# Small matmul groups of the mixers: fewer pauses between their halves, and row halves in alternation

## The chip, the cores and the metric

The kernel runs on one core of a Trainium2 chip. The metric is the device time of one execution in microseconds (us), from three runs of the kernel before: median 1280.27, lowest 1278.59, highest 1280.76. The engines of the core run side by side, each through its own instructions in program order: PE (TensorE, the matmuls), DVE (VectorE), ACT (ScalarE), POOL (GpSimd) and SP (which issues most DMAs). They wait for each other at semaphores.

## The reference

Two layers over 256 tokens of width 1024. Each layer adds half a SwiGLU FFN, a mixer and half a second FFN to the residual; a final RMSNorm follows. Cut to what matters here:

```python
for l in range(DEPTH):                      # DEPTH = 2
    x = x + 0.5 * swiglu(rmsnorm(x, ffn1_norm[l]), ...)
    h = rmsnorm(x, mix_norm[l])
    p = h @ w_in[l]                         # 1024 -> 8*256 + 4*1024
    u_a, u_b, r_p, k_p, v_p, z_in, b_g, c_g, gate_pre = jnp.split(p, SPLIT_POINTS, axis=-1)
    y_a = s5_mixer(u_a, ...)                # state space model, 16 groups
    y_b = pool_mixer(u_b, ...)
    y_c = rwkv7_mixer(h, r_p, k_p, v_p, ...)   # 4 heads of 64, delta rule
    y_d = short_conv_mixer(z_in, b_g, c_g, ...)
    branches = jnp.einsum('bsgc,gcd->bsgd', ys, w_branch[l])
    x = x + jnp.sum(branches * gates, axis=2).reshape(...) @ w_out[l]
    x = x + 0.5 * swiglu(rmsnorm(x, ffn2_norm[l]), ...)
return rmsnorm(x, final_norm)
```

`rwkv7_mixer` needs low-rank products for its decay, its learning rate and its gate, and a recurrence over time, which the kernel computes in four chunks of 64 tokens with small matrices for each head and chunk.

## The kernel before

**The main line.** Every large product (FFN, input projection, gates, branches, output) is made of float32r matmuls of 128 by 128 weights with 512 columns. A float32 operand is split into a high and a low part, so that each k-tile takes three matmuls (lines 256, 257, 258). I call these three a **tick**; the code calls `fl.tick()` after each. The weights come as units of two k-tiles: a DMA to `raw`, a conversion to `wh` on ACT (line 250), and the rest `wl` on DVE (line 225, the line of a helper that records every `tensor_tensor`).

**The side threads.** The mixer's branches are Python generators that are resumed between ticks while the program is being written, so the order of each engine's instructions is fixed by their `yield`s. `wA(n)` resumes before the products of the n-th step on (a step is two ticks of the same unit). `wM(n, banks)` resumes n ticks on, one such thread per tick, and only when so many of the four PSUM banks of the small products are free in this count. `Flow.tick` and `Flow._run` (lines 93 to 136) do this. An engine never leaves its order: what stands first and waits holds up all that is behind it.

**The small groups.** Between the ticks of each mixer PE also runs groups of small float32 matmuls. Names in the order in which they come, with the line of the matmul:

- `lr` (945): low-rank outputs, contraction over 64 rows for the first two and over 128 for the third; 256 columns each, two matmuls a group.
- `sT` (1352), `sY` (1397): input and output of S5. `sY` multiplies `U8` with `LK`, then the states `Hs` with `CA`, for four values of `u`.
- `gm` (1064): pair matrices of the four heads. Contraction over 64 rows: the upper half of the partitions for even heads, the lower half for odd ones. Its operands are `BK` and `W`. DVE masks the result into `Gm`; then POOL copies its diagonal blocks to `dg`, four copies per head (1073), and builds `Bl` and `Rd` from `dg`.
- `tmA`, `tmB` (1114, 1115): eight full transposes; DVE copies `tmA` to `RH`.
- `akv` (1138), `inv` (1093, 1171, 1183), `wu` (1202), `mq` (1228, 1229), `pn` (1243), `po` (1250), `zc` (1264), `pqz` (1282): the chunk recurrence, with 64 by 64 or 32 by 32 pieces.

Most of these groups are cut in two, three or four by a `yield wM()` in the middle of the loop: part, tick, part. The states `Hs` of S5 are made by DVE scans over `gB` and `gA`, two products on POOL (`gA`, `gB`), and a subtraction on DVE.

Of the kernel before, what the change touches and what calls it, by code (L numbers as in the profile page):

```python
# [50 lines left out]
def wA(n=1):  # L51
    """Resume before the products of the step n steps on."""
    return ("A", n, 0)


def wC(n=1):
    """As wA, after the conversion of weights."""
    return ("C", n, 0)


def wB(n=0, banks=0):
    """Resume after the products of the step n steps on, with so many PSUM banks free."""
    return ("B", n, banks)


def wT(n=1):
    """Resume n ticks on; a tick is between the products of two k-tiles."""
    return ("T", n, 0)


def wM(n=1, banks=0):
    """As wT, for products: one such thread goes on per tick, with so many PSUM banks free."""
    return ("M", n, banks)


class Flow:
    """Program order: a main line of product steps, and side threads resumed between them."""
# [94 lines left out]
def trunk_kernel(ctx: ExitStack, tc: tile.TileContext, a, out, dbg=None):  # L172
# [17 lines left out]
    # ------------------------------------------------------------- constants  # L190
# [16 lines left out]
    # ------------------------------------------------------------- helpers  # L207
# [22 lines left out]
    class Unit:  # L230
        """A block of weights: [128, nk, n] loaded, then split into two float32r parts."""
# [44 lines left out]
    # ------------------------------------------------------------- residual update and norm  # L276
# [20 lines left out]
    def next_input(t, hf, p, scale, ss, gain):  # L297
        """Thread: half hf of the residual of token tile t, its transpose times the next norm's gain in
        two parts, its sum of squares; the norm's factor follows with the second half and is applied
        to the products."""  # L300
# [23 lines left out]
    def last_norm(t, hf, p, scale, ss):  # L324
        """Thread: half hf of the result of token tile t; the second half scales both by the norm's factor."""
# [67 lines left out]
    # ------------------------------------------------------------- FFN  # L393
# [75 lines left out]
    # ------------------------------------------------------------- parameter columns  # L469
# [9 lines left out]
    def load_vecs(i, vr, first, after):  # L479
        """Thread: the rows of a group of parameters, as columns of vec."""  # L480
# [34 lines left out]
    # ------------------------------------------------------------- S5 preparation  # L515
# [120 lines left out]
    def s5_prepare(l, tp):  # L636
        """Matrices of layer l: boundary input LS, boundary output CA, in-block LK, phasor tables."""
# [16 lines left out]
        # B rows (re | im) and swapped; C rows, to be transposed  # L654
# [9 lines left out]
        # powers a^0..a^8  # L664
# [27 lines left out]
        # phasor tables e^{i theta 8 b}  # L692
# [14 lines left out]
        # B-bar rows (re | im) and swapped  # L707
# [11 lines left out]
        # C rows: X1 = (cre | -cim), X2 = (cim | cre)  # L719
# [70 lines left out]
    # ------------------------------------------------------------- mixer  # L790
    def mixer(l):
# [34 lines left out]
        def cols(names, mk):  # L826
            """512 columns of products with the layer input; then as two banks [128 ch, 2, S]."""
# [29 lines left out]
        class LowRank:  # L857
            """Rows of the low-rank input weights, and those times mu, side by side."""
# [42 lines left out]
        # ------------------------------------------------------- RWKV  # L901
        def rwkv():
# [19 lines left out]
            # low-rank outputs  # L922
# [18 lines left out]
            for i, (o_, nm) in enumerate(((sig, "rwkv_w0"), (aa, "rwkv_a0"), (gg, None))):  # L941
                yield wM(2 if i else 6, 1)
                p = bank("lr").rearrange("p (j t) -> p j t", j=2)
                for j in range(2):
                    pe.matmul(p[:, j], lhsT=lw[rows[i], i // 2, j * 128:(j + 1) * 128], rhs=z[rows[i], i // 2],  # L945
                              start=True, stop=True)
                yield wA(1)
                if nm:
                    for j in range(2):
                        sc.activation(o_[:, j], p[:, j], AF.Sigmoid, bias=col(l, nm, j))  # L950
                else:
                    sc.activation(o_, p, AF.Copy)
                free()
# [8 lines left out]
            # normalised removal key  # L962
# [35 lines left out]
            # decay products within chunks  # L998
# [28 lines left out]
            # scaled operands; slots: even chunk (a, v, r), odd chunk (v, a, r)  # L1027
# [23 lines left out]
            # pair matrices, [s, t]; rows (b|k) for even chunks, (k|b) for odd ones; columns (a | r)  # L1051
# [3 lines left out]
            for h in range(4):  # L1055
                yield wM(4 if h == 0 else 2, 1)
                j, e = h // 2, h % 2
                es = slice(64 * e, 64 * e + 64)
                p = bank("gm").rearrange("p (c t) -> p c t", c=4)
                for c in range(4):  # L1060
                    m, o = c // 2, c % 2
                    lhs = BK[es, 2 * j + m, 2 * o:2 * o + 2].rearrange("p k t -> p (k t)")
                    rhs = W[es, 2 * j + m, 0:3:2] if o == 0 else W[es, 2 * j + m, 4:6]
                    pe.matmul(p[:, c], lhsT=lhs, rhs=rhs, start=True, stop=True)
                yield wA(1)
                g_ = et([128, 4, 128], f"Gm{h}")
                tt(g_, p, maskb)
# [169 lines left out]
            for c in range(3):  # L1237
                if c:
                    yield wM()
# [447 lines left out]
```

## Time and profile before

| | |
|---|---|
| median of 3 runs | 1280.27 us |
| span of the profiled execution | 1278.3 us |
| PE busy | 1255.6 us (98%) |
| DVE, ACT, POOL busy | 760.9, 618.8, 388.5 us |
| mixer of layer 0 / of layer 1, up to the end of `pqz` | about 215 to 392 / 845 to 1021 us |

The profiled execution's own time is its span and what lies around it; the span is 2.0 us under the median of the runs. A busy share is time in which at least one instruction of the engine ran. Matmuls are pipelined, so the start times of the timeline tell more than the busy time: the main line's matmuls start 0.23 us apart, and a tick is 0.68 us.

### The profile page before, as it was taken

Reading aid. Unit: us, or ns where it says so; the run is one execution under the profiler, and the core shown is the slowest. Engines: PE = TensorE matmul, PEld = TensorE weight load, DVE = VectorE, ACT = ScalarE, POOL = GpSimd, SP = SyncE. Lnnn points to the kernel's source line nnn. Section 1 sums busy time; section 2 is a strip of 40 time slices with the busy share of each in tenths; the row PEclk is TensorE's granted clock in tenths of the full one; section 3 lists DMA queues with packets and bytes.
Section 4 is the critical chain, followed back from the end, with each engine's and each line's share of the span. In section 5 each row is a group of like instructions: output and inputs, shape, how many; then the busy total and the mean of one; then the engine's idle time right before and its main releaser. Section 6 shows DMA issues by size and latency. Waiting matters only on the chain.

```text
span 1278.3 us, 19253 instructions
## 1 busy us (share of the span) xinstructions
PE 1255.6 (98%) x7472; PEld 1013.3 (79%) x7472; DVE 760.9 (60%) x935; ACT 618.8 (48%) x787; POOL 388.5 (30%) x512
## 2 busy tenths in 40 slices
PE   7999999999999999999999999999999999999997
PEld 6888878876777788888888788878677787888886
DVE  6956557497547565554465565465965476655543
ACT  5454435655334454444354444365554354544433
POOL 4694383263123210000069453204612032000001
PEclk9999999998999999999999999999999999999999
DMA  8665656543444566656666566555244455666561
GB/s 257 179 219 179 184 159 183 166 135 121 126 133 145 176 182 187 191 176 188 190 187 195 170 186 188 153 188 178 96 134 133 133 165 165 212 184 180 182 197 66
DMA packets 139667, 216.29 MB, mean 169 GB/s; under 512 B 30092, under 2 KB 42232, under 8 KB 139576
## 3 DMA queue, kind: packets, MB, share of 16 engines
q1 hardware_dynamic: 138296, 213.63, 54.9%
q10 hardware_dynamic: 1120, 1.40, 0.3%
q8 instruction: 58, 0.95, 0.3%
q0 software_dynamic: 160, 0.05, 0.1%
q14 instruction: 33, 0.27, 0.1%
HBM read 212.29 MB, written 1.57 MB: 167 GB/s over the span
## 4 chain that ended last, share of the span: by engine, by line
PE 94%; DVE 4%; issue 0%; DMA 0%; ACT 0%; SPq 0%; POOLq 0%; POOL 0%; DVEq 0%; ACTq 0%
PE acc L256 29%; PE acc L258 28%; PE acc L257 28%; PE pb L268 3%; DVE wl L225 1%; PE inv L1093 1%; DVE cv L1506 1%; PE lr L945 0%; DMA x<-in_x_dram 0%; PE sY L1397 0%; DVE Gm L225 0%; PE wu L1202 0%; PE pb L771 0%; DVE mg L225 0%; PE po L1250 0%
## 5 line engine op out<-in xcount | busy, mean ns | idle before, releaser
L225 DVE TENSOR_TENSOR wl<-raw,wh 128x1024 fp32r<-128x1024 f32 (+1 forms) x390 | 492.2, 1263 | 300.0 <-ACT wh L250 297.7
L250 ACT ACTIVATE wh<-raw 128x1024 fp32r<-128x1024 f32 (+1 forms) x393 | 414.6, 1055 | 425.4 <-PE acc L258 390.7
L256 PE MATMUL acc<-wh,xh 128*128 128x512 f32 (+1 forms) x1248 | 494.7, 396 | 0.0
L258 PE MATMUL acc<-wh,xl 128*128 128x512 f32 (+1 forms) x1248 | 475.1, 381 | 0.0
L257 PE MATMUL acc<-wl,xh 128*128 128x512 f32 (+1 forms) x1248 | 474.5, 380 | 0.1
L256 PEld LDWEIGHTS acc<-wh,xh 128*128 128x128 f32 x1248 | 235.6, 189 | 49.1 <-issue 6.8
L258 PEld LDWEIGHTS acc<-wh,xl 128*128 128x128 f32 x1248 | 235.6, 189 | 45.5
L257 PEld LDWEIGHTS acc<-wl,xh 128*128 128x128 f32 x1248 | 236.1, 189 | 39.1 <-DVE wl L225 0.6
L258 PE MATMUL acc<-wh,hl 128*128 128x512 f32 x352 | 138.7, 394 | 0.0
L256 PE MATMUL acc<-wh,hh 128*128 128x512 f32 x352 | 138.2, 393 | 0.0
L257 PE MATMUL acc<-wl,hh 128*128 128x512 f32 x352 | 138.0, 392 | 0.0
L225 POOL TENSOR_TENSOR wl<-raw,wh 128x1024 fp32r<-128x1024 f32 x11 | 26.4, 2396 | 239.9 <-ACT wh L250 239.9
L256 PEld LDWEIGHTS acc<-wh,hh 128*128 128x128 f32 x352 | 66.1, 188 | 15.2 <-issue 1.3
L257 PEld LDWEIGHTS acc<-wl,hh 128*128 128x128 f32 x352 | 66.2, 188 | 14.6
L258 PEld LDWEIGHTS acc<-wh,hl 128*128 128x128 f32 x352 | 66.2, 188 | 13.3
L429 DVE SCALAR_TENSOR_TENSOR hd<-acc,rs,sg 128x512 f32<-128x512 f32 (+1 forms) x48 | 33.7, 703 | 38.4 <-PE acc L258 36.5
L333 POOL TENSOR_SCALAR pre<-ss 128x1 f32<-128x1 f32 x2 | 0.4, 221 | 173.7 <-ACT junk L281 173.7
L221 ACT ACTIVATE hh<-pb 128x512 fp32r<-128x512 f32 (+1 forms) x48 | 27.0, 563 | 45.5 <-PE pb L268 45.5
L222 DVE TENSOR_TENSOR hl<-pb,hh 128x512 fp32r<-128x512 f32 (+1 forms) x48 | 31.0, 646 | 27.9 <-ACT hh L221 27.6
L422 ACT ACTIVATE sg<-acc,rs 128x512 f32<-128x512 f32 (+1 forms) x48 | 31.1, 654 | 17.8 <-PE acc L258 16.8
L225 POOL TENSOR_TENSOR mg<-mg,gate 128x512 f32<-128x512 f32 x16 | 28.6, 1807 | 13.5 <-DVE gate L225 13.5
L314 ACT ACTIVATE xh<-xg 128x512 fp32r<-128x512 f32 x24 | 15.2, 632 | 30.6 <-DVE xg L225 30.5
(341 smaller groups left out, 1131.9 us busy)
## 6 DMA issues: line engine op xcount, KB each, us to landing
raw<-in_w_in_dram SPq DMA_DIRECT2D x96, 512.0 KB
raw<-in_ffn_w_up_dram SPq DMA_DIRECT2D x88, 512.0 KB
raw<-in_ffn_w_down_dram SPq DMA_DIRECT2D x88, 512.0 KB
raw<-in_ffn_w_gate_dram SPq DMA_DIRECT2D x87, 512.0 KB
raw<-in_w_branch_dram SPq DMA_DIRECT2D x16, 512.0 KB
raw<-in_w_out_dram SPq DMA_DIRECT2D x16, 512.0 KB
x<-in_x_dram SPq DMA_DIRECT2D x2, 512.0 KB
raw<-in_rwkv_g_dram SPq DMA_DIRECT2D x8, 128.0 KB
```

The costliest lines, as they stand in the source:

```text
L221: sc.activation(dh, src, AF.Copy)
L222: eng.tensor_tensor(out=dl, in0=src, in1=dh.bitcast(F32), op=ALU.subtract)
L225: eng.tensor_tensor(out=o, in0=i0, in1=i1, op=op)
L250: sc.activation(self.h, self.r, AF.Copy)
L256: pe.matmul(ps, lhsT=lh, rhs=wh, start=first, stop=False)
L257: pe.matmul(ps, lhsT=lh, rhs=wl, start=False, stop=False)
L258: pe.matmul(ps, lhsT=ll, rhs=wh, start=False, stop=last)
L268: pe.transpose(b[:, j * 128:(j + 1) * 128], src[:, j * 128:(j + 1) * 128], ident)
L314: sc.activation(dh, xg, AF.Copy)
L422: sc.activation(sg[:, :n], pg[:, :n], AF.Silu, scale=rstd[t])
L429: ve.scalar_tensor_tensor(out=hd[:, :n], in0=pu[:, :n], scalar=rstd[t], in1=sg[:, :n], op0=ALU.mult, op1=ALU.mult)
L1093: pe.matmul(p[qs, u], lhsT=lhs[qs, u], rhs=rhs[qs, u], start=True, stop=True)
```

## The change

It changes the order in which small products are written, and nothing in what is computed:

- in `akv`, `wu`, `mq`, `pn`, `pqz` and `sT` the `yield wM()` inside the loop goes, so that the parts stand behind each other; in `po` and `sY` four parts (of which `po` had two groups) become one and two;
- `lr`: the first two products share a turn, take two banks, and alternate between the row halves;
- `gm`: the heads come in pairs, two banks at once; the matmuls of the even and the odd head alternate, and `wM` is 4 for both pairs.

`inv` keeps its halves. Comments were removed too, so line numbers fall by a few.

```diff
-            for i, (o_, nm) in enumerate(((sig, "rwkv_w0"), (aa, "rwkv_a0"), (gg, None))):
-                yield wM(2 if i else 6, 1)
-                p = bank("lr").rearrange("p (j t) -> p j t", j=2)
+            for group in (((0, sig, "rwkv_w0"), (1, aa, "rwkv_a0")), ((2, gg, None),)):
+                yield wM(6 if group[0][0] == 0 else 2, len(group))
+                ps = [bank("lr").rearrange("p (j t) -> p j t", j=2) for _ in group]
                 for j in range(2):
-                    pe.matmul(p[:, j], lhsT=lw[rows[i], i // 2, j * 128:(j + 1) * 128], rhs=z[rows[i], i // 2],
-                              start=True, stop=True)
+                    for p, (i, _, _) in zip(ps, group):
+                        pe.matmul(p[:, j], lhsT=lw[rows[i], i // 2, j * 128:(j + 1) * 128], rhs=z[rows[i], i // 2],
+                                  start=True, stop=True)
...
-            for h in range(4):
-                yield wM(4 if h == 0 else 2, 1)
-                j, e = h // 2, h % 2
-                es = slice(64 * e, 64 * e + 64)
-                p = bank("gm").rearrange("p (c t) -> p c t", c=4)
+            for j in range(2):
+                yield wM(4 if j == 0 else 4, 2)
+                ps = [bank("gm").rearrange("p (c t) -> p c t", c=4) for _ in range(2)]
                 for c in range(4):
                     m, o = c // 2, c % 2
...
+                    for e in range(2):
+                        es = slice(64 * e, 64 * e + 64)
+                        lhs = BK[es, 2 * j + m, 2 * o:2 * o + 2].rearrange("p k t -> p (k t)")
+                        rhs = W[es, 2 * j + m, 0:3:2] if o == 0 else W[es, 2 * j + m, 4:6]
+                        pe.matmul(ps[e][:, c], lhsT=lhs, rhs=rhs, start=True, stop=True)
                 yield wA(1)
...
+                for e in range(2):
+                    h = 2 * j + e
+                    g_ = et([128, 4, 128], f"Gm{h}")
+                    tt(g_, ps[e], maskb)
+                    free()
...
             for h in range(4):
-                if h % 2 == 0:
-                    yield wM()
...
-                    if h2:
-                        yield wM()
...
-                    if j:
-                        yield wM()
...
             for c in range(3):
-                if c:
-                    yield wM()
...
-                if c % 2 == 0:
+                if c == 0:
                     yield wM()
...
-                if e:
-                    yield wM()
...
             for u in range(4):
-                if u == 2:
-                    yield wM()
...
             for u in range(4):
-                if u:
+                if u == 2:
                     yield wM()
```

What this does to the order of the built program, in layer 0; layer 1 has the same.

PE, at the pair matrices `gm`, between the transposes `bg` and `cg` of the input projection. Before:

```order
L823 MATMUL bg<-cst,tm 128x128 x4
L256 MATMUL acc<-wh,xh 128x512
L257 MATMUL acc<-wl,xh 128x512
L258 MATMUL acc<-wh,xl 128x512
L256 MATMUL acc<-wh,xh 128x512
L257 MATMUL acc<-wl,xh 128x512
L258 MATMUL acc<-wh,xl 128x512
L1064 MATMUL gm<-W,BK 128x128 x4
L256 MATMUL acc<-wh,xh 128x512
L257 MATMUL acc<-wl,xh 128x512
L258 MATMUL acc<-wh,xl 128x512
L823 MATMUL cg<-cst,tm 128x128 x4
```

After:

```order
L1066 MATMUL gm<-W,BK 128x128 x8
L256 MATMUL acc<-wh,xh 128x512
L257 MATMUL acc<-wl,xh 128x512
L258 MATMUL acc<-wh,xl 128x512
L823 MATMUL bg<-cst,tm 128x128 x4
L256 MATMUL acc<-wh,xh 128x512
L257 MATMUL acc<-wl,xh 128x512
L258 MATMUL acc<-wh,xl 128x512
L256 MATMUL acc<-wh,xh 128x512
L257 MATMUL acc<-wl,xh 128x512
L258 MATMUL acc<-wh,xl 128x512
L823 MATMUL cg<-cst,tm 128x128 x4
```

The first `gm` group has moved up by two ticks and the `bg` transposes, and holds two heads.

DVE, from the conversion behind `v` to `BK`, the last operand of `gm`. Before:

```order
L225 TENSOR_TENSOR wl<-raw,wh 128x1024
L1015 TENSOR_SCALAR kp<-aa,vec 128x256 x2
L1016 SCALAR_TENSOR_TENSOR kp<-kp,k 128x512
L1017 SCALAR_TENSOR_TENSOR bvec<-kk,aa 128x512
L1024 SCALAR_TENSOR_TENSOR rk<-r,vec,kp 128x256 x2
L225 TENSOR_TENSOR W<-kk,L_2551 128x4x2x64
L225 TENSOR_TENSOR wl<-raw,wh 128x1024
L225 TENSOR_TENSOR BK<-bvec,L_2552 128x4x2x64
L225 TENSOR_TENSOR W<-r,L_2551 128x8x64
L225 TENSOR_TENSOR BK<-kp,L_2552 128x4x128
```

After:

```order
L225 TENSOR_TENSOR wl<-raw,wh 128x1024
L225 TENSOR_TENSOR L_2543<-L_2542 128x512
L1017 TENSOR_SCALAR kp<-aa,vec 128x256 x2
L1018 SCALAR_TENSOR_TENSOR kp<-kp,k 128x512
L1019 SCALAR_TENSOR_TENSOR bvec<-kk,aa 128x512
L225 TENSOR_TENSOR wl<-raw,wh 128x1024
L1026 SCALAR_TENSOR_TENSOR rk<-r,vec,kp 128x256 x2
L225 TENSOR_TENSOR W<-kk,L_2542 128x4x2x64
L225 TENSOR_TENSOR BK<-bvec,L_2543 128x4x2x64
L225 TENSOR_TENSOR W<-r,L_2542 128x8x64
L225 TENSOR_TENSOR wl<-raw,wh 128x1024
L225 TENSOR_TENSOR BK<-kp,L_2543 128x4x128
```

Between `v` and `BK` there are now three conversions `wl`, where there were two; one that stood ahead of `v` has come behind it.

POOL, from the copies of the diagonal blocks to the products `gA` and `gB` for `Hs`; the number behind `Gm_` tells the heads apart. Before:

```order
L1073 COPY dg<-Gm_2706 32x64 x4
L1073 COPY dg<-Gm_2735 32x64 x4
L1073 COPY dg<-Gm_2756 32x64 x4
L1384 MEMSET Hs 128x16
L225 TENSOR_TENSOR gA<-gA,TC 128x512
L225 TENSOR_TENSOR gB<-gB,TS 128x512
L1073 COPY dg<-Gm_2783 32x64 x4
L225 TENSOR_TENSOR Bl<-dg,cst 128x256 x2
L225 TENSOR_TENSOR Rd<-Bl,cst 128x256
```

After:

```order
L1077 COPY dg<-Gm_2697 32x64 x4
L1077 COPY dg<-Gm_2703 32x64 x4
L1077 COPY dg<-Gm_2750 32x64 x4
L1077 COPY dg<-Gm_2756 32x64 x4
L225 TENSOR_TENSOR Bl<-dg,cst 128x256 x2
L225 TENSOR_TENSOR Rd<-Bl,cst 128x256
L1376 MEMSET Hs 128x16
L225 TENSOR_TENSOR gA<-gA,TC 128x512
L225 TENSOR_TENSOR gB<-gB,TS 128x512
```

The fourth head's copies, two `Bl` and `Rd` now stand ahead of `gA` and `gB`, with all 16 copies before them.

## Rows read from the trace of the kernel before

**Rows 1.** The page's chain by engine, and its group of weight conversions.
```profile
PE 94%; DVE 4%; issue 0%; DMA 0%; ACT 0%; SPq 0%; POOLq 0%; POOL 0%; DVEq 0%; ACTq 0%
...
L225 DVE TENSOR_TENSOR wl<-raw,wh 128x1024 fp32r<-128x1024 f32 (+1 forms) x390 | 492.2, 1263 | 300.0 <-ACT wh L250 297.7
```

**Rows 2.** Stretches, layers 0 and 1: busy PE, PEld, DVE, ACT, POOL; granted clock; DMA.
```profile
277.00:297.10 20.10, 16.81 (x96) 12.80 (x94) 19.96 (x27) 8.09 (x11) 13.43 (x20) 0.98 0.35 107
297.10:303.30 6.20, 6.16 (x39) 4.23 (x40) 2.57 (x4) 2.71 (x5) 2.29 (x4) 0.52 0.36 115
...
927.10:930.60 3.50, 3.19 (x28) 1.83 (x29) 2.05 (x5) 2.34 (x5) 2.56 (x4) 0.59 0.50 154
```

**Rows 3.** PE's timeline around `lr`: start us, length us, line, operation, last the idle time.
```profile
227.95 0.39 PE L258 MATMUL acc<-wh,xl 128*128 128x512 f32 x1
...
228.63 0.39 PE L258 MATMUL acc<-wh,xl 128*128 128x512 f32 x1
228.95 1.13 PE L945 MATMUL lr<-z,lw 64*128 64x256 f32 x4
...
230.58 0.39 PE L258 MATMUL acc<-wh,xl 128*128 128x512 f32 x1
...
233.91 0.39 PE L258 MATMUL acc<-wh,xl 128*128 128x512 f32 x1
234.13 1.02 PE L945 MATMUL lr<-z,lw 128*128 128x256 f32 x4
...
235.46 0.39 PE L258 MATMUL acc<-wh,xl 128*128 128x512 f32 x1
```

**Rows 4.** PE's timeline around a half of `akv`.
```profile
312.15 0.39 PE L258 MATMUL acc<-wh,yl 128*128 128x512 f32 x1
312.47 0.68 PE L1138 MATMUL akv<-UV,Gm 64*64 64x64 f32 x16
...
313.66 0.39 PE L258 MATMUL acc<-wh,yl 128*128 128x512 f32 x1
```

**Rows 5.** PE's timeline: the first `gm`, `tmA` between two ticks, the first `sY`.
```profile
277.85 1.13 PE L1064 MATMUL gm<-W,BK 64*128 64x128 f32 x8 [0.57 <-DVE BK L225]
...
291.37 0.40 PE L258 MATMUL acc<-wh,xl 128*128 128x512 f32 x1
...
292.94 0.40 PE L258 MATMUL acc<-wh,xl 128*128 128x512 f32 x1
...
293.96 0.43 PE L1397 MATMUL sY<-LK,U 128*32 128x128 f32 x8
297.14 0.66 PE L1397 MATMUL sY<-CA,Hs 128*32 128x128 f32 x8 [2.76 <-DVE Hs L225]
```

**Rows 6.** DVE's timeline from `v` to `Hs`.
```profile
262.79 0.87 DVE L917 SCALAR_TENSOR_TENSOR v<-v,vec 128x255 f32<-128x255 f32 x2 [0.16 <-ACT v L915]
...
277.03 0.68 DVE L225 TENSOR_TENSOR BK<-kp,L 128x512 f32<-128x512 f32 x1
...
281.88 0.69 DVE L225 TENSOR_TENSOR Gm<-gm,cst 128x512 f32<-128x512 f32 x1
...
296.38 0.70 DVE L225 TENSOR_TENSOR Hs<-gA,gB 128x496 f32<-128x496 f32 x1
```

**Rows 7.** POOL's timeline from the copies `dg` to `Rd`.
```profile
282.63 2.80 POOL L1073 COPY dg<-Gm 32x64 f32<-32x64 f32 x4 [8.42 <-DVE Gm L225]
285.73 4.87 POOL L1073 COPY dg<-Gm 32x64 f32<-32x64 f32 x8 [0.29 <-DVE Gm L225]
...
290.84 1.54 POOL L225 TENSOR_TENSOR gA<-gA,TC 128x512 f32<-128x512 f32 x1
292.35 1.50 POOL L225 TENSOR_TENSOR gB<-gB,TS 128x512 f32<-128x512 f32 x1
...
296.64 1.55 POOL L225 TENSOR_TENSOR Bl<-dg,cst 128x256 f32<-128x256 f32 x2
298.15 0.64 POOL L225 TENSOR_TENSOR Rd<-Bl,cst 128x256 f32<-128x256 f32 x1
```

More of the change, by code (lines that the diff above doesn't have):

```diff
@@ L940, in rwkv @@
             rows = (slice(0, 64), slice(64, 128), slice(0, 128))
-            for i, (o_, nm) in enumerate(((sig, "rwkv_w0"), (aa, "rwkv_a0"), (gg, None))):
-                yield wM(2 if i else 6, 1)
-                p = bank("lr").rearrange("p (j t) -> p j t", j=2)
+            for group in (((0, sig, "rwkv_w0"), (1, aa, "rwkv_a0")), ((2, gg, None),)):
+                yield wM(6 if group[0][0] == 0 else 2, len(group))
+                ps = [bank("lr").rearrange("p (j t) -> p j t", j=2) for _ in group]
                 for j in range(2):
-                    pe.matmul(p[:, j], lhsT=lw[rows[i], i // 2, j * 128:(j + 1) * 128], rhs=z[rows[i], i // 2],
-                              start=True, stop=True)
+                    for p, (i, _, _) in zip(ps, group):
+                        pe.matmul(p[:, j], lhsT=lw[rows[i], i // 2, j * 128:(j + 1) * 128], rhs=z[rows[i], i // 2],
+                                  start=True, stop=True)
                 yield wA(1)
[L948 to L953, printed above, removed]
+                for p, (_, o_, nm) in zip(ps, group):
+                    if nm:
+                        for j in range(2):
+                            sc.activation(o_[:, j], p[:, j], AF.Sigmoid, bias=col(l, nm, j))
+                    else:
+                        sc.activation(o_, p, AF.Copy)
+                    free()
             yield from until("r")
@@ L1054, in rwkv @@
             maskb = cc("mask").unsqueeze(1).to_broadcast([128, 4, 128])
-            for h in range(4):
-                yield wM(4 if h == 0 else 2, 1)
-                j, e = h // 2, h % 2
-                es = slice(64 * e, 64 * e + 64)
-                p = bank("gm").rearrange("p (c t) -> p c t", c=4)
+            for j in range(2):
+                yield wM(4 if j == 0 else 4, 2)
+                ps = [bank("gm").rearrange("p (c t) -> p c t", c=4) for _ in range(2)]
                 for c in range(4):
                     m, o = c // 2, c % 2
-                    lhs = BK[es, 2 * j + m, 2 * o:2 * o + 2].rearrange("p k t -> p (k t)")
-                    rhs = W[es, 2 * j + m, 0:3:2] if o == 0 else W[es, 2 * j + m, 4:6]
-                    pe.matmul(p[:, c], lhsT=lhs, rhs=rhs, start=True, stop=True)
-                yield wA(1)
-                g_ = et([128, 4, 128], f"Gm{h}")
-                tt(g_, p, maskb)
-                free()
-                Gm.append(g_)
-                gv = g_.rearrange("p (m o) s -> p o m s", o=2)
-                for q in range(4):
-                    qs, cs = slice(32 * q, 32 * q + 32), slice(32 * (q % 2), 32 * (q % 2) + 32)
-                    gp.tensor_copy(dg[qs, 2 * h:2 * h + 2], gv[qs, q // 2, :, cs])
+                    for e in range(2):
[3 more added lines that the diff above has]
+                        pe.matmul(ps[e][:, c], lhsT=lhs, rhs=rhs, start=True, stop=True)
+                yield wA(1)
+                for e in range(2):
+                    h = 2 * j + e
+                    g_ = et([128, 4, 128], f"Gm{h}")
+                    tt(g_, ps[e], maskb)
+                    free()
+                    Gm.append(g_)
+                    gv = g_.rearrange("p (m o) s -> p o m s", o=2)
+                    for q in range(4):
+                        qs, cs = slice(32 * q, 32 * q + 32), slice(32 * (q % 2), 32 * (q % 2) + 32)
+                        gp.tensor_copy(dg[qs, 2 * h:2 * h + 2], gv[qs, q // 2, :, cs])
             quarters = [(slice(32 * q, 32 * q + 32), q // 2, slice(32 * (q % 2), 32 * (q % 2) + 32)) for q in range(4)]
```

## The prediction

> **What bounds the kernel now.** I read the page's chain first: 94% of the time that decides the end is PE, 4% DVE [rows 1]. So whatever PE does not have to do is gained, except where PE waits for another engine. I then looked for such places, stretch by stretch, in the table of stretches and in PE's timeline. There is one per mixer. Between 277.0 and 297.1 us DVE is busy 19.96 of 20.10 us while PE is busy for 16.81 [rows 2]; PE waits there 0.57 us for `BK` at the first `gm` and 2.76 us for `Hs` at the first `sY` [rows 5]. Behind the second wait the granted clock is 0.52 for 6.2 us in layer 0 and 0.59 for 3.5 us in layer 1 [rows 2]: PE runs near the lower of its two levels, 1.2 GHz. The reader should see that this stretch belongs to a chain through DVE and POOL, and that before and behind it PE alone decides.
>
> **The price of a group.** From one line-258 matmul to the next, one tick takes 228.63 - 227.95 = 0.68 us. With `lr` of 64 rows in between it takes 230.58 - 228.63 = 1.95, so the group costs 1.27; with `lr` of 128 rows 235.46 - 233.91 = 1.55, so 0.87 [rows 3]. Both stream the same columns, so a group in small tiles costs about 0.40 us beside its streaming. A half of `akv` costs 313.66 - 312.15 - 0.68 = 0.83 [rows 4], of which 0.43 is left; it streams 8 x 64 = 512 columns, as `lr` does in 0.87. So matmuls that alternate between row and column halves overlap two by two.
>
> **The change part by part, per mixer.**
> Starts saved, at 0.40 each: `lr` 1, `sT` 1, `gm` 2, `sY` 2, `akv` 1, `wu` 2, `mq` 2, `pn` 2, `po` 1, `pqz` 1, which is 15 x 0.40 = 6.0.
> Overlap of row halves: `lr` and `gm` alternate in rows only and share their columns, which the trace of before does not show. The bounds: nothing, if only separate columns overlap, or half of the streaming, as in `akv`, the nearest row. I take half: 0.87 for `lr`, and 2 x 0.87 for `gm` (four matmuls of 128 columns each, the same 512 columns). Taken by itself PE thus gets 8.6 us less work per mixer, 17.2 in both.
> On this a page has a word against the trace: the Trainium skill, "TensorEngine Tiling (Array Packing)", section "Restrictions and Gotchas", says that different row tiles cannot use the same PSUM bank at the same time. `akv` writes one bank from both halves, and its row shows the overlap all the same; `lr` and `gm` get a bank for each half, so by either reading they overlap.
>
> **Where the first part of it goes.** All of `lr`, `sT`, `gm` lies ahead of the wait for `Hs`, so what counts there is when `Hs` comes. I follow that chain.
> DVE starts it with `v` at 262.79 [rows 6]. In the changed order `v` comes one tick earlier (0.68) and behind a cheaper `lr` (0.40 + 0.87): 1.95 earlier. But one more conversion `wl`, 1.26 us [rows 1], stands between `v` and `BK`. `BK` ends at 277.03 + 0.68 = 277.7 now, so then at 277.7 - 1.95 + 1.26 = 277.0. PE stands at the first `gm` now at 277.85 - 0.57 = 277.3; then two ticks, the dearer `lr` and a start of `sT` earlier, 1.36 + 1.27 + 0.40 = 3.0, and also ahead of `bg`: at 274.3 or before. The wait for `BK` grows from 0.6 to about 3 us.
> From the end of `BK` to `Gm` DVE has the same seven steps, 4.2 us (277.7 to 281.9). So `Gm` and the first copy `dg` come 0.7 earlier, the copy at 281.9.
> On POOL, now, 12 copies run from 282.63 to 290.6, 0.66 each, and then `gA` and `gB` at 1.5 each end at 293.85; `Hs` is not held by them, DVE gets to it at 296.38 [rows 6, 7]. In the changed order all 16 copies (10.6), two `Bl` (1.5) and `Rd` (0.6) stand ahead: 281.9 + 12.7 = 294.6; with a short memset and `gA` and `gB` (3.2) 297.8; `Hs` 0.7 more: 298.5. POOL is blocked by work that nobody needs yet, and `Hs` is 1.4 us later than the 297.1 of now. PE is at `sY` long before: it gets there now at 293.96 for the first half.
> Behind `Hs` PE then has one tick more to do than now (0.68), the second eight transposes less, which now come before `sY` (292.94 - 291.37 - 0.68 = 0.89 [rows 5]), and two starts of `sY` less (0.80). Together: +1.4 + 0.7 - 0.9 - 0.8 = +0.4 us. Of the 5.0 us saved up to here nothing is left.
> Does DVE hold `Hs` longer? In its order two small copies `RH` come ahead of `Hs` and one product behind it; it would be at `Hs` about as much earlier as its chain starts earlier, so POOL is what is late last.
>
> **What is left.** Behind `sY` PE alone decides: `akv` 1, `wu` 2, `mq` 2, `pn` 2, `po` 1, `pqz` 1, nine starts or 3.6 us. Waits that these groups have for ACT and DVE are covered by ticks as now; the distances in ticks between `wu`, `mq` and `zc` shrink by one at most. Sum per mixer: 0.4 - 3.6 = -3.2 us; both: -6.4. The profiled execution would have a span of 1278.3 - 6.4 = 1271.9; the median of the runs lies 2.0 above that span, so 1273.9.
>
> **Rivals.**
> *A. Everything saved is gained.* It needs `BK` and `Hs` to come 3 us and more earlier than DVE and POOL can have them. 1280.3 - 17.2 = 1263.1. Against it speak both waits in both layers, and a DVE that is full there. A chance of 0.05. The Trainium skill, "TensorEngine Tiling (Array Packing)", section "PSUM Bottleneck", warns of it in general: tiling makes the matmuls faster, not the work that empties PSUM. `Gm` is that work here; by that rule it is my forecast and not A.
> *B. POOL is not late*, as its copies speed up where DVE pauses, and `Hs` moves with DVE's chain, 1.9 us earlier rather than 1.4 later: -3.2 - 3.3 = -6.5 per mixer, 1267.3. 0.13.
> *C. Row halves don't overlap*, so the change does not do what it says for `lr` and `gm`: `v` and all behind it 0.87 later, 2.3 left per mixer: 1275.6. 0.10.
> *D. The clock takes the rest.* The two waits of PE become longer. If half speed at `gm` delays the second pair of heads, and so POOL's copies and `Hs`, or lasts longer behind `Hs`, the cost is up to what it is now once more: 6.2 x (1 - 0.52) = 3.0 us per mixer. That leaves 0.2 of 3.2: 1279.9. 0.14.
> *E. Slower.* The same mechanism, from `gm` to the end of `sY` in one piece: the clock falls in the 3 us wait for `BK`, PE does two ticks, `gm`, `bg` and `cg` at half speed, the heads 2 and 3 come about 2 us later, `Hs` with them, and the stretch behind `Hs`, six ticks and `sY` or about 6 us, runs wholly at half speed, 3 us more than now. +5 - 3.2 = +1.8 per mixer: 1283.9. It decides from 3.2 us of loss on; what speaks against it is that PE has spare time between `gm` and `Hs`, so that the first half speed is mostly hidden. 0.07.
>
> **How the numbers follow.** My forecast, with `Hs` 1 to 2 us late: 0.51, at 1273.9; by itself it spans 1271 to 1277. The range takes in C, most of B and part of D: 1267.5 to 1279.0. About 0.2% is what a measurement of this kernel can tell from no change. Faster by more than that: forecast, A, B and C, 0.79. Within: D, 0.14. Slower: E, 0.07.
>
> **What would show it.** In the profile of the changed kernel PE should wait some 3 us for `BK` at the first `gm` and 4 us or more for `Hs` at `sY`, with POOL's `gB` ending just before `Hs`. A group in small tiles should still cost 0.40 beside its streaming, and the first `lr` group, with four matmuls, 1.27. From the end of `sY` to `pqz` the mixer should be 3.6 us shorter, and from its start to the end of `sY` not shorter at all. Wrong is the forecast if the waits for `BK` and `Hs` do not grow, if DVE and not POOL is last before `Hs`, or if a new wait of PE appears between `akv` and `pqz`.

## The result and the profile after

The changed kernel takes 1268.69 us (median of 4 runs, 1266.79 to 1271.31), the kernel before 1279.43 in the same comparison: a ratio of 0.9923, 95% interval 0.9907 to 0.9938. That is 8 to 12 us less; I had forecast 6.4. The profiled execution has a span of 1267.2 us, 11.1 less than before.

The chain of the page and the weight conversions, against [rows 1]:

```profile
PE 93%; DVE 4%; issue 1%; POOL 1%; DMA 1%; ACT 0%; POOLq 0%; SPq 0%; DVEq 0%; ACTq 0%
...
L225 DVE TENSOR_TENSOR wl<-raw,wh 128x1024 fp32r<-128x1024 f32 (+1 forms) x390 | 498.0, 1278 | 302.1 <-ACT wh L250 294.4
```

PE still decides; new in the chain are 1% each of POOL, DMA and issue, which before rounded to 0.

**Where the time went.** Both kernels have the same 1664 ticks, so a mixer can be cut at the same ticks. I use three marks: the line-258 matmul just ahead of `lr` (228.63 before [rows 3], 228.91 after), the first matmul of `sY` with `Hs` (297.14 [rows 5], 297.75), and two line-258 matmuls further on, which I call X (76 ticks behind the first mark, behind `sY`; in the changed kernel `akv` follows it) and Y (99 ticks on, behind `pqz`). PE's timeline of after at these places, with the waits (columns as in [rows 3]):

```profile
228.91 0.39 PE L258 MATMUL acc<-wh,xl 128*128 128x512 f32 x1
229.23 1.13 PE L946 MATMUL lr<-z,lw 64*128 64x256 f32 x8
...
230.87 0.39 PE L258 MATMUL acc<-wh,xl 128*128 128x512 f32 x1
...
277.40 2.08 PE L1066 MATMUL gm<-W,BK 64*128 64x128 f32 x16 [2.94 <-DVE BK L225]
...
295.90 0.43 PE L1389 MATMUL sY<-LK,U 128*32 128x128 f32 x8
297.75 0.43 PE L1389 MATMUL sY<-CA,Hs 128*32 128x128 f32 x8 [1.43 <-DVE Hs L225]
...
305.79 0.39 PE L258 MATMUL acc<-wh,xl 128*128 128x512 f32 x1
...
399.35 0.39 PE L258 MATMUL acc<-wh,xl 128*128 128x512 f32 x1
...
920.74 0.32 PE L1389 MATMUL sY<-CA,Hs 128*32 128x128 f32 x4 [2.47 <-DVE Hs L225]
```

The pieces between the marks, in us, for layers 0 and 1, worked out from such rows of each trace:

| kernel | start to `Hs` | `Hs` to X | X to Y |
|---|---|---|---|
| before | 68.51, 68.50 | 11.61, 10.43 | 97.21, 97.21 |
| after | 68.84, 68.47 | 8.04, 9.60 | 93.56, 93.56 |
| e1: only the groups behind `sY` | 68.51, 68.49 | 10.33, 11.62 | 93.58, 93.59 |
| e2: only `lr`, `sT`, `gm`, `sY` | 68.55, 68.50 | 8.09, 9.55 | 97.14, 97.15 |
| e3: `lr` and `gm` without alternation | 69.12, 69.56 | 8.08, 8.09 | 93.56, 93.56 |
| e4: `gA` and `gB` first on POOL | 68.74, 68.95 | 8.09, 8.09 | 93.56, 93.55 |
| e11: `lr` as before | 66.44, 66.45 | 11.16, 11.15 | 93.53, 93.52 |
| e12: the waits filled | 68.48, 68.48 | 8.05, 8.05 | 93.56, 93.56 |

(In e11 one tick and eight transposes, 0.68 + 0.89 us, lie behind `Hs` that in after lie ahead of it; its whole mixer, start to Y, takes 171.1 us, as after does with 170.4 and 171.6.) The reader should see three things. Up to `Hs` nothing was gained, and at most 0.3 us lost (before, after, e1, e2). From X to Y it is 3.6 us in every pair. And the piece in the middle swings by 1.2 to 1.6 us between the two layers of one execution, which run the same order: before and e1 are the same up to X and show 11.6 and 10.4 in either order of the layers. Between two layers, from Y to the next first mark, it is 452.9 us everywhere; only the first DMAs of the kernel add a swing of their own (the first mark lies between 227.9 and 229.4).

**What the middle piece swings by is the clock.** Stretches of after (columns as in [rows 2]): from the first `gm`, then from `Hs`, of layer 0; the same of layer 1.

```profile
277.30:285.00 7.70, 7.60 (x36) 6.33 (x36) 7.63 (x11) 0.52 (x1) 2.65 (x5) 0.58 0.46 138
297.70:304.00 6.30, 6.25 (x75) 4.83 (x76) 4.83 (x7) 3.59 (x9) 0.00 (x0) 1.00 0.28 86
900.00:907.00 7.00, 6.24 (x36) 5.15 (x36) 6.93 (x12) 0.56 (x1) 1.34 (x4) 0.76 0.38 105
920.70:929.00 8.30, 8.26 (x77) 6.13 (x78) 6.83 (x10) 4.62 (x9) 0.00 (x0) 0.79 0.37 102
```

The clock now falls behind the wait for `BK`, where PE has time to spare until `Hs`. In layer 0 it stays low there for longer (0.58), PE reaches `sY` late, waits only 1.43 us, and the clock is full behind it; before it was 0.52 there [rows 2]. In layer 1 it recovers sooner, PE waits 2.47 us at `sY`, and the clock falls once more (0.79 over the stretch).

**What was last before `Hs`.** DVE, ACT and POOL of after, layer 0 (DVE rows answer [rows 6], POOL rows [rows 7]):

```profile
290.61 1.00 DVE L1498 SCALAR_TENSOR_TENSOR cv<-zc,vec,cv 128x255 f32<-128x255 f32 x2
291.58 0.42 DVE L1123 COPY RH<-tmA 64x256 f32<-64x256 f32 x1
292.01 0.43 DVE L1124 COPY RH<-tmA 64x256 f32<-64x256 f32 x1
293.75 2.91 DVE L1498 SCALAR_TENSOR_TENSOR cv<-zc,vec,cv 128x255 f32<-128x255 f32 x2 [1.32 <-ACT cv L1496]
296.59 1.11 DVE L225 TENSOR_TENSOR Hs<-gA,gB 128x496 f32<-128x496 f32 x1
```

```profile
292.55 0.38 ACT L1125 ACTIVATE UV<-tmA 64x256 f32<-64x256 f32 x1 [1.50 <-POOL Bl L225]
292.94 0.38 ACT L1126 ACTIVATE UV<-tmA 64x256 f32<-64x256 f32 x1
293.22 0.50 ACT L1496 ACTIVATE cv<-zc,vec 128x256 f32<-128x256 f32 x1
```

```profile
282.18 4.80 POOL L1077 COPY dg<-Gm 32x64 f32<-32x64 f32 x8 [8.42 <-DVE Gm L225]
287.31 4.39 POOL L1077 COPY dg<-Gm 32x64 f32<-32x64 f32 x8 [0.33 <-DVE Gm L225]
291.79 1.26 POOL L225 TENSOR_TENSOR Bl<-dg,cst 128x256 f32<-128x256 f32 x2
293.00 0.65 POOL L225 TENSOR_TENSOR Rd<-Bl,cst 128x256 f32<-128x256 f32 x1
...
293.66 1.28 POOL L225 TENSOR_TENSOR gA<-gA,TC 128x512 f32<-128x512 f32 x1
294.90 1.48 POOL L225 TENSOR_TENSOR gB<-gB,TS 128x512 f32<-128x512 f32 x1
```

POOL is done with `gB` at 296.38. DVE gets to `Hs` at 296.59, and that because of a detour: `RH` now stands ahead of the second half of `cv` on DVE; ACT copies `UV` out of the same bank behind `RH` and `cv`'s first step behind `UV`; DVE's `cv` waits 1.32 us for that, and `Hs` stands behind `cv`. The idle time of ACT is put down to `Bl`, but `UV` starts 0.1 us behind the end of `RH`, and in the kernel before the same wait of `UV` is put down to `RH`. Layer 1 shows the same: `gB` ends at 919.37, `Hs` starts at 919.57, behind the same wait of 1.32 us.

### The profile page after: what moved, and what is told of

Read it like the earlier page. It is cut to its first block, busy times and chain, and to the rows that moved or that the text cites. A ratio compares the mean times of both kernels' runs of the same rounds, so it can differ in the third digit from the quotient of the medians.

```text
span 1267.2 us, 19245 instructions
## 1 busy us (share of the span) xinstructions
PE 1241.1 (98%) x7472; PEld 1011.4 (80%) x7472; DVE 759.2 (60%) x935; ACT 618.7 (49%) x787; POOL 385.1 (30%) x512
## 4 chain that ended last, share of the span: by engine, by line
PE 93%; DVE 4%; issue 1%; POOL 1%; DMA 1%; ACT 0%; POOLq 0%; SPq 0%; DVEq 0%; ACTq 0%
PE acc L256 29%; PE acc L258 28%; PE acc L257 28%; PE pb L268 3%; PE inv L1097 1%; DVE wl L225 1%; POOL dg L1077 1%; DVE cv L1498 1%; DVE W L225 0%; PE sY L1389 0%; PE pb L771 0%; DVE rk L1026 0%; DVE mg L225 0%; DMA vr<-in_ffn_norm_dram 0%; PE wu L1202 0%
## 5 line engine op out<-in xcount | busy, mean ns | idle before, releaser
L225 DVE TENSOR_TENSOR wl<-raw,wh 128x1024 fp32r<-128x1024 f32 (+1 forms) x390 | 498.0, 1278 | 302.1 <-ACT wh L250 294.4
```

What stands on the lines that cost most here:

```text
L225: eng.tensor_tensor(out=o, in0=i0, in1=i1, op=op)
```

## The experiments

All changes are against the changed kernel unless said otherwise. Ratios are against the kernel before, with 95% intervals.

**e1 and e2: the change in two.** e1 is the kernel before with only the edits of `akv`, `wu`, `mq`, `pn`, `po`, `pqz`; e2 the kernel before with only those of `lr`, `sT`, `gm`, `sY`.

> Only the groups behind sY are changed (akv, wu, mq, pn, po, pqz); lr, sT, gm and sY stand as before. Theory: nine starts of 0.40 us are saved per mixer, nothing in this part waits, and the part up to the end of sY stays as it was: 3.6 us per mixer, 7.2 in both, so about 1272.2 where before gives 1279.4. Rival 1 (the gain of the whole change comes mostly from the early groups): under 4 us. Rival 2 (the whole change is these groups alone, the early ones are worth nothing, and the rest of the measured 10 us is a matter of where the clock falls): 7 us in the time, but 10 in a profile that happens to have no fall of the clock behind sY.

> Only lr, sT, gm and sY are changed; the groups behind sY stand as before. Theory: Hs comes 0 to 0.4 us later than before against the start of the mixer, behind it PE has one tick more, eight transposes and two starts less (1.0 us), so 0.7 to 1.0 us are gained per mixer where the clock falls behind sY as before, and up to 3 us more where it does not: 1279.4 less 1.5 to 4.5, 1275 to 1278. My prediction on record: a loss of 0.4 per mixer, 1280.2. Rival (all the work saved is gained): 5.0 us per mixer, 1269.4.

Measured: e1 1273.05 us, ratio 0.9964 (0.9951 to 0.9976); e2 1275.99 us, 0.9989 (0.9977 to 1.0001), beside 1278.13 of before. In e1's trace X to Y is 3.63 us shorter per mixer, 7.2 in both, as expected; its time fell by 3 to 6 us only. The granted clocks of the runs show where the rest is: e1's five runs have 0.994 to 0.996, and of the 17 runs of before in this comparison eight have 0.995 or 0.996 and nine 0.998 or 0.999. Beside those eight e1's mean span is 6.6 us shorter (1270.6 against 1277.2). Why all of e1's runs have the lower clock and only half of those of before, whose program is the same up to X, stays open. e2's time lies in the expected range, though its interval still takes in no change, and the table shows why: `Hs` comes neither later nor earlier. My forecast of a loss for this half (1280.2) fell, and so did the rival of 5.0 us per mixer.

**e3: no alternation inside the groups.**

```diff
-                for j in range(2):
-                    for p, (i, _, _) in zip(ps, group):
+                for p, (i, _, _) in zip(ps, group):
+                    for j in range(2):
                         pe.matmul(p[:, j], ...            # lr
...
-                for c in range(4):
-                    for e in range(2):
+                for e in range(2):
+                    for c in range(4):
                         pe.matmul(ps[e][:, c], ...        # gm
```

> The changed kernel, with the same groups at the same places, but inside lr and gm the matmuls of one row half come first and then those of the other: nothing alternates there. Theory: row halves overlap, so in the trace the lr group costs 1.27 + 0.87 = 2.1 us instead of 1.28 and the second gm group 2.1 instead of 1.30. On the path lies only the 0.87 of lr, as it moves v and with it DVE's chain to Hs; gm is hidden in the time until Hs: +0.9 per mixer, about 1270.4 where the changed kernel gives 1268.7. Rival 1 (there is no overlap of row halves): the groups cost the same and the time is the same. Rival 2 (gm is on the path too): +2.6 per mixer, 1273.9.

Measured: 1268.7 us, ratio 0.9931 (0.9919 to 0.9943), as the changed kernel. The timeline of e3:

```profile
228.72 0.39 PE L258 MATMUL acc<-wh,xl 128*128 128x512 f32 x1
229.04 1.14 PE L946 MATMUL lr<-z,lw 64*128 64x256 f32 x8
...
230.68 0.39 PE L258 MATMUL acc<-wh,xl 128*128 128x512 f32 x1
...
285.39 1.71 PE L1066 MATMUL gm<-W,BK 64*128 64x128 f32 x16
```

My expectation was wrong in one half: `lr` costs 230.68 - 228.72 - 0.68 = 1.28 us without any alternation. Two matmuls of one half in a row still overlap with the two of the other; it is enough that they stand in one group. With four in a row (`gm`) the length goes from 1.16 to 1.71. My theory had this hidden, which it is not fully: the first `gm`, at half speed, lasts 3.06 us in both layers, DVE in layer 0 waits 0.52 us for `tmA` ahead of `RH`, and `Hs` comes 0.3 and 1.1 us later than after. But behind `sY` the clock is 1.00 in both layers, and the piece to X takes 8.08 and 8.09. From the start to X that makes 77.2 and 77.7 us, beside 76.9 and 78.1 of after: two effects cancel, and the time stays.

**e4, e5: `Hs` earlier.** In e4 POOL makes `gA` and `gB` ahead of the last eight copies `dg`; in e5 `Hs` also stands ahead of `RH` and of the second half of `cv` on DVE.

```diff
-                    gv = g_.rearrange("p (m o) s -> p o m s", o=2)
-                    for q in range(4): ... gp.tensor_copy(dg[...], gv[...])
+                    if j == 0:
+                        dcopy(h)             # the same four copies
...
                 sc.activation(UVv[0:64, 1, hs], pr_[0:64, 1], AF.Copy)
+                if j == 0:
+                    dcopy(2); dcopy(3); B0 = lvl(0); Bl = lvl(1)
+                    tt(Rd, B0, id32, ALU.add, eng=gp)
...
-            yield wA(3)
+            yield wA(2)                      # e5 only: Hs one step earlier
```

> The changed kernel, with POOL's copies dg of heads 2 and 3, two Bl and Rd put behind gA and gB; DVE's order is unchanged, Hs still stands behind the second half of cv. Theory: DVE is last before Hs, since cv waits 1.3 us for ACT and ACT for DVE's RH; POOL ends only 0.2 to 0.3 us ahead of it. Then Hs comes 0.3 us earlier by the wait, and up to 1.5 us earlier if cv runs faster when gA and gB are not beside it: 0.6 to 3 us in the time, 1266 to 1268. Rival (POOL is last, as my prediction had it): Hs comes up to 4 us earlier, PE waits for it no longer, and the clock does not fall behind sY: 3 us per mixer, about 1262.7.

> As the run with gA and gB first on POOL, and Hs one step earlier on DVE: ahead of RH and of the second half of cv, no longer behind the wait of cv for ACT. Theory: in the changed kernel DVE's order is what holds Hs (RH, the wait of 1.3 us for ACT, cv 1.4 to 2.9 us stand ahead of it), so Hs comes some 4 us earlier, PE finds it ready at sY, the wait of 1.4 to 2.5 us is gone and no half speed follows it: about 2 us per mixer, 1264.5 where the changed kernel gives 1268.7. Rival (DVE as a whole is full, and what is moved behind Hs only holds PE somewhere else, at the weights wl or at akv): less than 1 us in the time.

Measured: e4 1269.36 us, ratio 0.9931 (0.9917 to 0.9945); e5 1268.96, 0.9921 (0.9906 to 0.9936): neither gains anything. e4 has `Hs` at 68.74 and 68.95 us behind the start, beside 68.84 and 68.47 after. So POOL's end was not what held it, and my prediction's reason fell. POOL's products do count in another way, as DVE and POOL of e4 show, layer 0:

```profile
290.00 2.03 DVE L1506 SCALAR_TENSOR_TENSOR cv<-zc,vec,cv 128x255 f32<-128x255 f32 x2
...
294.12 1.42 DVE L1506 SCALAR_TENSOR_TENSOR cv<-zc,vec,cv 128x255 f32<-128x255 f32 x2 [1.32 <-ACT cv L1504]
```

```profile
288.96 2.28 POOL L225 TENSOR_TENSOR gB<-gB,TS 128x512 f32<-128x512 f32 x1
```

The second half of `cv`, no longer beside `gA` and `gB`, takes 1.42 us instead of 2.91, as the theory hoped; but the first half, now beside `gB`, takes 2.03 instead of 1.00, and the `wl` ahead of it 1.96 instead of 1.21. The slow piece has only moved.

In e5 `Hs` did come 3.8 and 3.7 us earlier (65.05, 64.82), as the theory said, and the time did not move, as its rival had it, but for the most part for another reason:

```profile
293.61 0.71 DVE L225 TENSOR_TENSOR Hs<-gA,gB 128x496 f32<-128x496 f32 x1
...
296.41 1.27 DVE L1506 SCALAR_TENSOR_TENSOR cv<-zc,vec,cv 128x255 f32<-128x255 f32 x2 [1.31 <-ACT cv L1504]
```

```profile
294.38 0.42 PE L1397 MATMUL sY<-CA,Hs 128*32 128x128 f32 x8 [0.70 <-DVE Hs L225]
...
309.86 0.33 PE L1102 MATMUL inv<-Tm,Bl 32*32 32x32 f32 x17 [1.44 <-DVE Tm L1140]
```

With `Hs` the code also moves `sY` three ticks forward and ahead of the second `tmA`, so PE has 3 x 0.68 + 0.89 = 2.9 us more to do behind `Hs`; of 3.7 us that leaves 0.8, and the work that DVE and POOL put off now makes PE wait 1.44 us at `inv` in layer 0. In layer 1 PE waits 1.82 us for `Hs`, and the clock is 0.86 in the 11.8 us behind it. What counts is not when `Hs` comes but `Hs` plus what PE still has to do behind it.

**e6: `gm` later.**

```diff
-                yield wM(4 if j == 0 else 4, 2)
+                yield wM(8 if j == 0 else 4, 2)
```

> The changed kernel with the first gm group four ticks later, and all that follows it by its ticks (second gm, the transposes tmA and tmB, akv and on); sY keeps its place. Theory: the wait of 2.9 us for BK at gm is gone, and with it the half speed there, but Hs hangs on DVE alone and comes when it came: PE is at sY some 4 us earlier and waits there 5 to 6 us, with half speed behind it. The time is the same within 1 us per mixer, 1267 to 1271. Rival (the wait at gm and the half speed behind it are on the path): 2.9 + 1.5 us per mixer are gained, about 1260.

Measured: 1263.68 us, ratio 0.9881 (0.9867 to 0.9896): 5 us faster than the changed kernel. Theory and rival both missed. PE's and DVE's timelines of e6:

```profile
277.70 1.16 PE L1066 MATMUL gm<-W,BK 64*128 64x128 f32 x16 [0.47 <-DVE gt L225]
...
284.85 1.97 PE L1066 MATMUL gm<-W,BK 64*128 64x128 f32 x14 [2.62 <-DVE Gm L225]
...
294.00 0.43 PE L1389 MATMUL sY<-CA,Hs 128*32 128x128 f32 x8 [0.16 <-DVE Hs L225]
```

```profile
292.62 0.69 DVE L225 TENSOR_TENSOR cv<-cv,bg 128x512 f32<-128x512 f32 x1
293.23 0.71 DVE L225 TENSOR_TENSOR Hs<-gA,gB 128x496 f32<-128x496 f32 x1
```

`tmA` moves with `gm`, so `RH` and `UV` leave the place ahead of `cv`, and the detour over ACT is gone: `Hs` 65.98 us behind the start, 2.5 to 2.9 earlier than after, with `sY` at the same tick; 0.9 of that goes to the second eight transposes, which now stand behind `sY`. The wait at the first `gm` became one of 2.62 us at the second, where PE waits for `Gm` to free a PSUM bank, and the clock falls there (0.67 from 284.8 to 290.0 us); that is hidden until `Hs`, for which PE waits 0.16 us.

**e7: `inv` in whole groups.**

```diff
                 for u in range(8):
-                    if u == 4:
-                        yield wM()
                     for qs, _, _ in quarters:
...
```

> The changed kernel, with the two halves of each product inv of the block doubling in one group too (eight groups instead of sixteen). Theory: behind sY PE alone decides and a start costs 0.40 us, so the price of a start is the same here: 0.59 + 0.59 become 0.78, eight starts per mixer, 3.2 us, 6.4 in both: 1262.3 where the changed kernel gives 1268.7. Rival (the chain of the inverse, PE to ACT to PE to DVE to PE, is what decides there, and it has fewer ticks between its steps): waits appear at inv and less than 3 us are gained.

Measured: 1263.53 us, ratio 0.9882 (0.9867 to 0.9897). No wait appears, but the price is another:

```profile
308.02 0.40 PE L258 MATMUL acc<-wh,xl 128*128 128x512 f32 x1
308.35 0.75 PE L1095 MATMUL inv<-Tm,Bl 32*32 32x32 f32 x64
...
309.60 0.40 PE L258 MATMUL acc<-wh,xl 128*128 128x512 f32 x1
```

A whole group costs 309.60 - 308.02 - 0.68 = 0.90 us, two halves 2 x 0.59 to 0.60: 0.29 saved per group, 2.3 per mixer, not 3.2. The 0.40 of a start is not the same for pieces of 32 by 32.

**e8, e9, e10: together.** e8 has e5, e6 and e7; e9 only e6 and e7. e10 is e9 with the second `gm` at `wM(8, 2)`, the first `tmA` at `wM(4, 2)` and `sY` at `wM(8, 1)`.

> The three edits together: Hs early, gm four ticks later, inv whole. Theory: with Hs early the wait at gm is no longer hidden in the time until Hs, so that gm later earns too: 2 (Hs) + 3 (inv) + 2 to 4 (gm and the half speed behind it) per mixer, 1251 to 1255. Rival (DVE is full from v to Hs): only Hs and inv earn, about 1258.

> Of the three edits tried together the two that earned: gm four ticks later and inv whole; Hs and the copies dg in the order that the changed kernel's code gives. Theory: the two lie in different stretches (ahead of Hs, and behind akv) and add up: 1263.7 less 2.3 to 2.4 per mixer (what a whole inv group took less in the trace, 8 x 0.29) is 1259.0. Rival (earlier ends of the first part only meet a later engine, as when Hs was put early): one of the gains is lost, 1261 to 1264.

> As the one before, with the second gm group four ticks later as well (eight behind the first), the first transposes tmA four ticks behind it, and sY three ticks later. Theory: the wait of 2.6 us of the second gm for Gm (its PSUM bank) and the half speed behind it go, and as sY moves with it no wait takes their place: 2 to 4 us per mixer, 1251 to 1255. Rival (DVE is full from v to Hs and sets the pace there, whatever PE's order is): waits for wl or for Hs take their place, and the time is within 2 us of 1259.

Measured: e8 1264.51 us, ratio 0.9886 (0.9870 to 0.9903); **e9 1259.53 us, 0.9847 (0.9835 to 0.9860)**, the best version; e10 1260.51 us, 0.9855 (0.9842 to 0.9868). e8 missed both expectations for the reason seen in e5: `Hs` comes at 65.2 us, only 0.8 earlier than in e6, but 2.9 us of PE's work are moved behind it, and PE waits for it 2.32 and 1.09 us. e9 is the sum of two gains in different stretches, as expected. In e10 the wait that I took away came back at another place, at the same engine:

```profile
295.11 0.52 PE L1387 MATMUL sY<-LK,U 128*32 128x128 f32 x8 [3.96 <-DVE Gm L225]
```

`sY` now stands behind the second pair `Gm` for a PSUM bank. There DVE sets the pace, as the rival had it, though the rival looked for the wait at `wl` or `Hs`.

**e11: `lr` as before.** The hunk of `lr` is undone; the rest of the change stays.

> The changed kernel with lr as before: three groups, the first two of 64 rows each, so that v and all that hangs on it by ticks is one tick later, and PE spends 1.27 us more per mixer. Theory: what lr gains ahead of v is eaten on DVE, where the earlier v puts one wl more ahead of BK (1.2 us) and RH and the wait of cv for ACT (0.85 + 1.3 us) ahead of Hs; with lr as before these go, Hs comes no later, and the time stays within 1.5 us of the changed kernel's 1268.7. Rival (lr's 1.27 us per mixer are on the path): 1271.2 or more.

Measured: 1268.7 us, ratio 0.9918 (0.9904 to 0.9933), the time of the changed kernel. `lr` alone brings nothing that can be measured: without it `v` comes later, but `Hs` comes 2.0 to 2.4 us earlier, since on DVE it stands ahead of `RH`, and `cv` has no wait:

```profile
291.28 2.93 DVE L1496 SCALAR_TENSOR_TENSOR cv<-zc,vec,cv 128x255 f32<-128x255 f32 x4
294.12 0.71 DVE L225 TENSOR_TENSOR Hs<-gA,gB 128x496 f32<-128x496 f32 x1
...
295.93 0.41 DVE L1121 COPY RH<-tmA 64x256 f32<-64x256 f32 x1
```

The clock takes part here: behind `Hs` it is 0.85 over 11.1 us in both layers, so that `Hs` to X takes 11.16 us where 8.05 + 0.68 + 0.89 = 9.62 would be an estimate at full clock (8.05 is measured in e12). Without that fall e11's mixer would take some 169.6 us, and the changed kernel's takes 170.1 without one (e12): it is not `lr` that makes the changed kernel faster.

**e12: work in place of waiting.** The added matmuls compute nothing that is used.

```diff
...
+                if j == 0:
+                    for _ in range(3):
+                        pe.matmul(pg2[0], lhsT=ident, rhs=x[0][:, :512], start=True, stop=True)   # ahead of gm
...
+            for _ in range(3):
+                pe.matmul(pY_, lhsT=ident, rhs=x[0][:, :512], start=True, stop=True)              # ahead of sY
```

> The changed kernel with three matmuls of 512 columns, whose result is overwritten, ahead of the first gm group and three ahead of sY, 2.6 us each, so that PE is busy where it waits for BK and for Hs. Nothing else is changed. Theory: the clock falls because PE stands still there; kept busy it stays at its upper level behind gm and behind sY, Hs comes when it came, and the pieces from pool to the end of sY take the same in both layers, 32.9 to 33.4 us instead of 33.1 and 34.3: about 1267.5, and the runs lie closer together than the 4.5 us of the changed kernel. Rival 1 (the clock falls for another reason): granted clocks of 0.5 to 0.6 stay where they were. Rival 2 (the added matmuls are themselves on the path): 2 us per mixer and more are lost, 1273.

Measured: 1266.29 us (1265.57 to 1267.01), ratio 0.9899 (0.9886 to 0.9912). By the medians that is 2.4 us faster than the changed kernel, by useless work. The intervals of the two ratios just overlap; the two traces give 1.9 us (start to Y 340.2 for both layers against 342.1). The runs lie within 1.4 us instead of 4.5, but so do the five of e3, whose waits are not filled; of a smaller scatter these few runs are no proof. Timeline and stretches of e12, layer 0:

```profile
273.86 2.74 PE L1063 MATMUL gm<-x,cst 128*128 128x512 f32 x6
276.88 1.16 PE L1070 MATMUL gm<-W,BK 64*128 64x128 f32 x16 [0.28 <-DVE BK L225]
...
292.83 2.74 PE L1389 MATMUL sY<-x,cst 128*128 128x512 f32 x6
...
296.95 0.43 PE L1396 MATMUL sY<-CA,Hs 128*32 128x128 f32 x8 [1.03 <-DVE Hs L225]
```

```profile
277.00:285.00 8.00, 7.98 (x59) 6.39 (x60) 7.93 (x12) 1.55 (x2) 3.04 (x6) 1.00 0.42 133
297.00:303.00 6.00, 6.00 (x74) 4.62 (x75) 4.53 (x7) 3.36 (x7) 0.00 (x0) 1.00 0.31 90
```

The granted clock is 1.00 behind both places, `Hs` comes at 68.48 us in both layers, and `Hs` to X takes 8.05 in both. So where PE does not stand still, the clock does not fall, and the fall is the whole swing of the middle piece: wherever the clock behind `Hs` is 1.00 with this order on PE (layer 0 of after and of e2, both layers of e3, e4 and e7), the piece takes 8.04 to 8.09 too. But not every wait brings a fall. In layer 0 of e4 PE waits 2.45 us for `Hs`, and behind it the clock is 1.00:

```profile
296.60:303.00 6.40, 6.39 (x75) 4.93 (x76) 4.92 (x7) 4.74 (x9) 0.46 (x1) 1.00 0.30 84
```

After 2.47 us in layer 1 of after it fell. What decides between the two, no run here shows.

## Why the prediction was right in sign and short in size

**The price of a group: right.** Nine starts behind `sY` are 3.6 us on paper and 3.6 in the traces (97.21 to 93.56 is 3.65, e1 gives 3.63, e2 against after 3.58). The groups one by one: `akv` 2 x 0.83 to 1.29, `wu` 1.24 for 2 x 0.80, `mq` 1.35 for 2 x 0.87.

**Row halves overlap: right.** `lr` with four matmuls costs 230.87 - 228.91 - 0.68 = 1.28, as much as two did [rows 3]; a `gm` group of eight costs at full clock what one of four did, 1.30. Rival C is refuted.

**The wait for `BK` grows to about 3 us: right**, 2.94 in both layers. What PE saves ahead of `Hs` is swallowed: right too. The start to `Hs` is 68.5 us before and 68.5 to 68.8 after, and e11 shows that `lr` brings nothing.

**The wait for `Hs` grows to 4 us or more: wrong.** It shrank from 2.76 to 1.43 and 2.47 us. `Hs` came hardly later, and PE came to `sY` later than before: 67.4 and 66.0 us behind the start instead of 65.7, held up by the wait of 2.94 us at `gm` and the half speed behind it.

**`Hs` 1.4 us later: the first failed step.** It came 0.3 us later in layer 0 and not at all in layer 1, so the term of +1.4 measures 0.0 to 0.3. I had costed POOL's copies at 0.66 each, with the pause between them, and 15.9 us from the first copy to the end of `gB`; they took 0.57 (9.19 for 16), and the way 14.2 (282.18 to 296.38). And I had excluded DVE ("POOL is what is late last"), the very sign that I had named as making the forecast wrong. I had counted its instructions ahead of `Hs`, two small copies more and one product less, but not that the second half of `cv` stands behind them and waits for ACT, which waits for those copies. The engine that I costed was nearly last, and another, which I had let go, was last by 0.2 us. POOL held `Hs` only by way of DVE: beside `gA` and `gB` the second half of `cv` took 2.91 us.

**What PE has left behind `Hs`: right as work, wrong as time.** One tick more, eight transposes and two starts less are 1.0 us. But I let the half speed behind `Hs` stand as it was, and put its change only on the losing side (rivals D and E). At full clock the piece takes 8.05 us in the changed kernel (e12), so by estimate 8.05 - 0.68 + 0.89 + 0.80 = 9.06 in the one before; measured were 10.4 to 11.6 before and 8.0 to 9.6 after. The fall cost 1.94 us per mixer on average before (four pieces, of before and e1) and 0.77 after (of after and e2). In these traces this is a second failed term: 1.2 us per mixer that stand at nothing in the sum. The wait moved to `gm`, where a fall of the clock is nearly free: `Hs` comes at 68.84 and 68.47 us behind it, and at 68.48 in e12, where there is none.

Together per mixer: about 0 at `Hs` instead of -1.4, 1.0 for the work, 1.2 for the clock, 3.6 behind: 5.8 instead of 3.2, which is 11.6 for both layers beside 11.1 in the two spans. Without the clock it is 4.6, or 9.2 for both layers, and that lies within the 8 to 12 us of the ratio as well. The clock's share holds for the traces, not for every execution: six of the 17 runs of before beside e1 have a granted clock of 0.999 and a mean span of 1273.4 us, the eight at 0.995 and 0.996 one of 1277.2. The four runs of e12, at 0.998 and 0.999, have 1264.5, which is 8.9 less than those six. So the step at `Hs`, 2.8 us in both mixers, is the main part of what my sum lacked; how much the clock adds to the medians stays open.

The time is near rival B's 1267.3, but not by its sum: `Hs` did not come 1.9 us earlier.

**On the bank.** The Trainium skill, "TensorEngine Tiling (Array Packing)", section "PSUM Bottleneck", says that tiling speeds up TensorE but not what empties PSUM. That fits e6 and e10, where 2.62 and 3.96 us of PE's waiting are for DVE's `Gm`; there the place of `Gm` in DVE's order makes it late, as two `Gm` take only 1.28 us in both.

## What to carry to other kernels

Where a chain on another engine sets the next meeting point, work saved on PE ahead of it was worth nothing here: cost the meeting point plus what PE still has to do behind it, and follow every instruction that stands ahead of it in each queue, with whom that one waits for. A wait of PE can cost the clock behind it as well, so ask where a wait will lie, not only how long it is; ahead of a later wait a fall was nearly free here (0.4 us at most). Merging small groups earns where PE alone decides, at a price per start that has to be read for each tile shape.

## What the runs showed of the hardware that I had not expected

- Useless matmuls in two waits per mixer kept the granted clock at 1.00 and made the kernel about 2 us faster (1.9 in the traces, 2.4 by the medians).
- Matmuls of different row halves overlap without alternating, if few stand in a row: 2 + 2 of 256 columns cost 1.28 us in either order, 4 + 4 of 128 columns are 1.16 long alternated and 1.71 not.
- DVE and POOL slow each other down. In the changed kernel two `cv` of DVE take 2.91 us beside `gA` and `gB` of POOL, and the two before them 1.00 beside copies `dg`; in e4, where `gA` and `gB` stand earlier, the long and the short pair change places (2.03 and 1.42), and `gB` itself takes 2.28 us instead of 1.48. `Hs` takes 1.11 us beside a `Bl` and 0.71 in e5, e6 and e11, beside copies `dg`. The Trainium skill, "SBUF — State Buffer", section "SBUF: two separate sides", says that the two share a port pair which a GpSimd instruction, or a DVE instruction with two SBUF inputs, holds for its whole length while the other is blocked; that agrees with the rows beside POOL's products, but beside the copies little of it is seen, and no run here took the cause apart.
